# The first projection of a recurrent encoder: 256 of 1024 channels multiplied before the RMSNorm

## The chip, the cores and the metric

The kernel runs on one core of a Trainium2 chip. The time is the device time of one execution in microseconds (us); of the kernel before, three runs were timed, and their median is 829.23 us. All instruction times are read from one profiled execution, counted from the start of its span. The engines are PE (matrix products, with its weight loads listed apart as PEld), DVE (vector), ACT (scalar), POOL (GpSimd) and SP, which issues most of the DMA.

## The reference

One encoder layer over 512 tokens of 1024 channels, float32, with a residual stream `x`:

```python
n = rmsnorm(x, norm_mix)                 # x * rsqrt(mean(x*x) + 1e-6) * norm_mix
proj = n @ w_in + b_in                   # 1024 -> 4624 columns: q, forget gates, values, gates of two head groups
x += concat(hgrn2(proj), mlstm(proj)) @ w_out
x += cross_attention(rmsnorm(x), rmsnorm(mem))
x += square(relu(rmsnorm(x) @ w_up)) @ w_down
out = rmsnorm(x, norm_final)
```

The columns 1536 to 2047 of `proj` are the values of the HGRN2 heads, `v = n @ w_in[:, 1536:2048] + b_in[1536:2048]`. They are computed first, and the change lies in their computation and in what prepares it. Since 1/rms is one number for each token and `norm_mix` one for each channel, `(x * r * g) @ W` equals `r * (x @ (g * W))`, with `r` applied to rows of the result and `g` to rows of `W`; over a part of the channels too.

## The kernel before

**Products.** A float32 product is made of three passes over pairs of rounded tiles: `split_out` lets ACT write the high part of a tile (a rounded copy) and DVE the low part (the tile less its high part); `mm3` then issues high·high, high·low and low·high (lines 261, 262 and 263). Every weight block (128 x 1024, 512 KB) is loaded by SP into one of three buffers `st`, and split by `split(i)` into one of three buffers `wh` and one of three `wl` (line 258: ACT, then DVE). A block can be split only when PE has done its last product with the block three before it.

**The first projection.** The tokens are four tiles of 128 (t = 0 to 3), the channels eight groups of 128 (k). A tile of `x` comes by one DMA of 512 KB. `x_stat(t)` sums its squares (ACT, line 338; for tile 0 half on ACT, half on DVE) and POOL makes 1/rms by a power of -0.5 (line 340). `x_scale(t, g)` multiplies 512 channels by 1/rms and by `gmix[g]` on DVE (line 344); `gmix` is the row `norm_mix` spread over the partitions by PE (`spread`, line 164). `x_turn(t, g)` transposes these four 128 x 128 blocks on PE (line 349) against the identity in `cs`, and `x_split(t, g)` splits the result into `xT` (line 258). `part_v(t, q)` then multiplies two channel groups of tile t by weight block q: 6 matmuls of 512 columns into the accumulator `acc_v[t]`. The last blocks (q = 3) and the bias are outside the hand order: `d = acc_v[t] + bias` on DVE (line 429). `xT` is kept: the gate projection (lines 617, 618) and all later projections of `proj` multiply it as well.

**What sets the order.** Inside `manual_schedule` PE, DVE and ACT take their work in the written order; the calls are interleaved so that one tile's transposes stand between other tiles' products. POOL and SP, and everything after the block, are put in order by the scheduler of the framework. Each engine runs its instructions strictly in that order; an instruction that waits holds all that is behind it. Before the first transposes `keep_busy` issues products of a constant tile (line 160) that nothing reads.

The order before, of which the change rewrites all:

```python
x_stat(0); x_scale(0, 0); x_turn(0, 0); spread(1); split(0); x_split(0, 0); x_stat(1)
part_v(0, 0); x_scale(1, 0); x_turn(1, 0); split(1); x_stat(2); part_v(0, 1); ...
```

Of the kernel before, what the change touches and what calls it, by code (L numbers as in the profile page):

```python
# [39 lines left out]
C_ID, C_MF, C_MB, C_SEL, NC1 = 0, 128, 256, 384, 392  # L40
# [40 lines left out]
def trunk(ctx: ExitStack, tc: tile.TileContext, x, mem, wpk, vec, cst, lmask, rmask, rows, out):  # L81
    nc = tc.nc
# [4 lines left out]
    v, sc, gp, pe = nc.vector, nc.scalar, nc.gpsimd, nc.tensor  # L87
# [33 lines left out]
    cs = sb.tile([P, NC1], F32, name="cs")  # L121
# [19 lines left out]
    def behind(a, b):  # L141

        tc.add_manual_dep(a.ins, b.ins.name, mybir.DependencyInfo(mybir.DependencyClass.NoSync, mybir.DependencyReason.DATA),
                          reason="order of an engine")

    def load_x(t):
        nc.sync.dma_start(out=xtile[t], in_=x[t * P:t * P + P, :])

    row_load = nc.scalar.dma_start(out=grow1[96:97, :], in_=rows[0:1, :])
    load_x(0)  # L150
    behind(nc.scalar.dma_start(out=cs, in_=cst[:, 0:NC1]), row_load)
    for g in range(2):
        v.memset(grow1[0:96, g * 512:g * 512 + 512], 0.0)
    gmix = [smb(), smb()]
    idle = mmb()

    def keep_busy(n):

        for _ in range(n):
            pe.matmul(idle[:, 0:P], lhsT=ones[:, 0:P], rhs=ones[:, 0:P], start=True, stop=True)  # L160

    def spread(g):

        pe.matmul(gmix[g], lhsT=ones[0:97, 0:P], rhs=grow1[0:97, g * 512:g * 512 + 512], start=True, stop=True)

    with tc.manual_schedule(engines={mybir.EngineType.PE}):
        keep_busy(6)
        spread(0)
        keep_busy(4)

    def small_setup():
        lmf = A4()
        nc.sync.dma_start(out=vc, in_=vec)
        nc.sync.dma_start(out=lmf[:, 0:len(LEVELS) * P], in_=lmask)
        for j in range(4):
            a = lmf[32 * j:32 * j + 32, 32 * j:NLV * P]
# [53 lines left out]
    st_tiles, hl_tiles = {}, {}  # L230

    def load(i):
        if i >= NSTREAM or i in st_tiles:
            return
        t = T("st", 1024, 3)
        nc.sync.dma_start(out=t, in_=wpk[i])
        st_tiles[i] = t

    def split(i):
        if i >= NSTREAM or i in hl_tiles:  # L240
            return
        load(i)
        s = st_tiles[i]
        hi, lo = T("wh", 1024, 3, F32R), T("wl", 1024, 3, F32R)
        made = split_out(hi, lo, s)
        hl_tiles[i] = (hi, lo)
        return made[1]
# [9 lines left out]
    def split_out(dst_hi, dst_lo, src):  # L257
        return sc.activation(dst_hi, src, AF.Copy), v.tensor_tensor(out=dst_lo, in0=src, in1=dst_hi.bitcast(F32), op=ALU.subtract)  # L258

    def mm3(ps, ah, al, bh, bl, first, last):  # L260
        pe.matmul(ps, lhsT=ah, rhs=bh, start=first, stop=False)  # L261
        pe.matmul(ps, lhsT=ah, rhs=bl, start=False, stop=False)  # L262
        pe.matmul(ps, lhsT=al, rhs=bh, start=False, stop=last)  # L263
# [50 lines left out]

    xT = XT()
    xs = xk(xT)
    load(0)
    load_x(1)
    load(1)
    load_x(2)  # L320
    load_x(3)
    load(2)
    load(3)

    junk, junk0 = xT[1][:, 0:1025], G4()
    rx, tp = {}, {}

    def x_stat(t):

        ss = tiny(1)  # L330
        if t == 0:
            s0, s1 = tiny(1), tiny(1)
            sc.activation(junk[:, 512:1025], xfull[t][:, 512:1025], AF.Square, scale=1.0 / 32, accum_out=s1)
            xg = xfull[t][:, 0:512]
            v.scalar_tensor_tensor(out=junk0[:, 0:512], in0=xg, scalar=1.0 / D, in1=xg, op0=ALU.mult, op1=ALU.mult, accum_out=s0)
            v.tensor_tensor(out=ss, in0=s0, in1=s1, op=ALU.add)
        else:
            sc.activation(junk, xfull[t], AF.Square, scale=1.0 / 32, accum_out=ss)
        rx[t] = tiny(1)
        gp.tensor_tensor(out=rx[t], in0=ss, in1=nh, op=ALU.pow)  # L340

    def x_scale(t, g):
        xg = xtile[t][:, g * 512:g * 512 + 512]
        v.scalar_tensor_tensor(out=xg, in0=xg, scalar=rx[t], in1=gmix[g], op0=ALU.mult, op1=ALU.mult)

    def x_turn(t, g):
        tp[t, g] = smb()
        for k in range(4):
            pe.transpose(tp[t, g][:, k * P:k * P + P], xtile[t][:, g * 512 + k * P:g * 512 + k * P + P], ident)

    def x_split(t, g):
        p3 = tp[t, g][:, :].rearrange("p (k t) -> p k t", t=P)
        split_out(ap(xT[g], t * P, [1024, 4], [1, P]), ap(xT[g], 512 + t * P, [1024, 4], [1, P]), p3)

    acc_v = [mmb() for _ in range(4)]

    def part_v(t, q):
        w = hl_tiles[q]  # L360
        for k in range(2):
            kk = 2 * q + k
            z = slice(k * 512, k * 512 + 512)
            mm3(acc_v[t], xs[kk][0][:, t * P:t * P + P], xs[kk][1][:, t * P:t * P + P], w[0][:, z], w[1][:, z], kk == 0, kk == 7)

    ET = mybir.EngineType
    with tc.high_priority(), tc.manual_schedule(engines={ET.PE, ET.DVE, ET.Activation}):
        x_stat(0)
        x_scale(0, 0)
        x_turn(0, 0)  # L370
        spread(1)
        split(0)
        x_split(0, 0)
        x_stat(1)
        part_v(0, 0)
        x_scale(1, 0)
        x_turn(1, 0)
        split(1)
        x_stat(2)
        part_v(0, 1)  # L380
        x_split(1, 0)
        x_scale(2, 0)
        part_v(1, 0)
        x_turn(2, 0)
        x_stat(3)
        x_scale(3, 0)
        part_v(1, 1)
        x_turn(3, 0)
        x_scale(0, 1)
        x_split(2, 0)  # L390
        x_scale(1, 1)
        part_v(2, 0)
        x_split(3, 0)
        x_turn(0, 1)
        split(2)
        part_v(2, 1)
        x_split(0, 1)
        x_turn(1, 1)
        x_scale(2, 1)
        part_v(3, 0)  # L400
        x_split(1, 1)
        x_scale(3, 1)
        part_v(3, 1)
        x_turn(2, 1)
        x_split(2, 1)
        part_v(0, 2)
        x_turn(3, 1)
        x_split(3, 1)
        part_v(1, 2)
        part_v(2, 2)  # L410
        split(3)
        part_v(3, 2)
        small_setup()


    vh = []

    def bias_row(i):
        b = T2()
# [3 lines left out]
    bvh = bias_row(0)  # L423
    load(4)
    load(5)
    for t, ps in enumerate(acc_v):
        part_v(t, 3)
        d = VV()
        v.tensor_tensor(out=d[:, 0:512], in0=ps, in1=bvh[:, 0:512], op=ALU.add)
        vh.append(d)  # L430


    ys = [None] * 8
# [1029 lines left out]
```

## Time and profile before

| | us |
|---|---|
| median of three timed runs (lowest, highest) | 829.23 (829.09, 829.29) |
| profiled execution, its own time | 829.61 |
| its span from first to last instruction | 827.6 |
| PE busy in the span | 814.7 |
| DVE, ACT, POOL busy | 590.6, 435.2, 77.7 |
| first transposes of `x` on PE start | 7.36 |
| the ten small products of line 656 start on PE | 54.20 |

The page gives busy time by engine, the chain of work that ended last (followed back from the last instruction to what released it), and groups of instructions. The timeline lists single instructions: start, duration, engine, line, operation, tiles, shape; in brackets the idle time before it and what ended that. A PE matmul of the timeline lasts longer than it holds the engine, since the next one starts before it has drained: what counts for throughput is the distance from start to start. The products of line 656 serve as a mark below: the same work stands ahead of them on PE in both kernels, apart from what the change adds, and from there on all engines have the same instructions in the same order.

### The profile page before, as it was taken

The numbers are of one execution on the slowest core, as the hardware profiler recorded it, in microseconds if no ns is written. First come the engines' busy times: TensorE is split into PE (matmuls) and PEld (weight loads), VectorE is DVE, ScalarE is ACT, GpSimd is POOL, SyncE is SP. The second block draws the span as 40 slices with busy tenths as digits, with TensorE's granted clock in tenths as the row PEclk, the third lists the DMA queues.
The fourth block names the chain that finished last, engine by engine and source line by source line (L and its number), as shares of the span: only waits on it lengthen the run. The fifth ranks groups of instructions, "written<-read, shape, count | busy, mean of one in ns | idle before, by whom it ended". The sixth has DMA issues, their size and how long they took to land.

```text
span 827.6 us, 12644 instructions
## 1 busy us (share of the span) xinstructions
PE 814.7 (98%) x4862; PEld 677.0 (82%) x4862; DVE 590.6 (71%) x1046; ACT 435.2 (53%) x791; POOL 77.7 (9%) x131
## 2 busy tenths in 40 slices
PE   8999999999999999999999999999999999999996
PEld 6788778877878988887888888888888888888885
DVE  6568975699479888545668985676568566756685
ACT  5247574546578485445455575443454345434544
POOL 2000000100010000100100004012102210220001
PEclk9999999999999999999999999999999999999998
DMA  7332223322342334532343349969836982798332
GB/s 277 118 116 94 78 79 104 101 88 81 102 128 77 128 128 152 148 96 89 106 124 72 83 126 305 254 166 272 224 101 182 280 207 94 187 295 204 105 74 101
DMA packets 34125, 118.91 MB, mean 144 GB/s; under 512 B 3921, under 2 KB 4049, under 8 KB 34066
## 3 DMA queue, kind: packets, MB, share of 16 engines
q1 hardware_dynamic: 22832, 77.80, 27.6%
q0 software_dynamic: 10944, 39.85, 21.7%
q8 instruction: 38, 0.62, 0.3%
q10 hardware_dynamic: 290, 0.47, 0.2%
q14 instruction: 21, 0.17, 0.1%
HBM read 116.00 MB, written 2.10 MB: 143 GB/s over the span
## 4 chain that ended last, share of the span: by engine, by line
PE 85%; issue 6%; DVE 5%; ACT 2%; DMA 1%; POOL 1%; POOLq 0%; ACTq 0%; DVEq 0%
PE mm L261 17%; PE mm L263 17%; PE mm L262 17%; PE sm L1154 6%; PE sm L1155 6%; PE sm L1153 6%; PE mm L1154 2%; PE mm L1153 2%; PE mm L1155 2%; PE sm L827 1%; DVE wl L258 1%; PE sm L562 1%; PE sm L485 1%; ACT wh L258 1%; PE sm L263 1%
## 5 line engine op out<-in xcount | busy, mean ns | idle before, releaser
L258 ACT ACTIVATE wh<-st 128x1024 fp32r<-128x1024 f32 x131 | 138.7, 1060 | 185.0 <-PE mm L262 117.4
L261 PE MATMUL mm<-xT,wh 128*128 128x512 f32 x544 | 215.5, 397 | 0.0
L258 DVE TENSOR_TENSOR wl<-st,wh 128x1024 fp32r<-128x1024 f32 x131 | 160.1, 1223 | 77.3 <-ACT wh L258 76.8
L263 PE MATMUL mm<-xT,wl 128*128 128x512 f32 x544 | 212.9, 391 | 0.1
L262 PE MATMUL mm<-xT,wh 128*128 128x512 f32 x544 | 212.5, 391 | 0.2 <-DVE xT L975 0.2
L263 PEld LDWEIGHTS mm<-xT,wl 128*128 128x128 f32 x544 | 102.2, 188 | 21.8 <-DVE wl L258 0.3
L262 PEld LDWEIGHTS mm<-xT,wh 128*128 128x128 f32 x544 | 102.3, 188 | 20.8 <-DVE xT L975 0.9
L261 PEld LDWEIGHTS mm<-xT,wh 128*128 128x128 f32 x544 | 102.2, 188 | 20.8 <-ACT wh L258 0.3
L1102 POOL DMA_DIRECT2D as<-in_wpk x52 | 39.6, 763 | 250.0 <-DVE wl L258 165.0
L1342 DVE SCALAR_TENSOR_TENSOR t<-mm,rg 128x512 f32<-128x512 f32 x32 | 22.0, 690 | 52.2 <-PE mm L263 52.0
L1155 PE MATMUL sm<-wh,yT 128*128 128x512 f32 x128 | 49.8, 389 | 0.0
L1154 PE MATMUL sm<-wl,yT 128*128 128x512 f32 x128 | 49.8, 389 | 0.0
L1153 PE MATMUL sm<-wh,yT 128*128 128x512 f32 x128 | 49.8, 389 | 0.0
L258 ACT ACTIVATE wh<-as 128x1024 fp32r<-128x1024 f32 x26 | 27.6, 1062 | 37.0 <-PE sm L1155 23.7
L258 DVE TENSOR_TENSOR wl<-as,wh 128x1024 fp32r<-128x1024 f32 x26 | 31.9, 1225 | 14.0 <-ACT wh L258 14.0
L1153 PE MATMUL sm<-wh,a 128*128 128x512 f32 x84 | 32.9, 391 | 0.0
L1155 PE MATMUL sm<-wh,a 128*128 128x512 f32 x84 | 32.7, 390 | 0.0
L1154 PE MATMUL sm<-wl,a 128*128 128x512 f32 x84 | 32.7, 389 | 0.0
L1285 DVE TENSOR_TENSOR vv<-vv,sm 128x512 f32<-128x512 f32 x48 | 31.0, 680 | 1.7 <-PE sm L1155 1.7
L199 POOL TENSOR_TENSOR tiny<-tiny,misc 128x4 f32<-128x4 f32 (+1 forms) x10 | 9.6, 963 | 201.9 <-DVE tiny L197 136.7
L1153 PEld LDWEIGHTS sm<-wh,yT 128*128 128x128 f32 x128 | 24.0, 188 | 5.0
L1155 PEld LDWEIGHTS sm<-wh,yT 128*128 128x128 f32 x128 | 24.0, 188 | 5.0
(329 smaller groups left out, 1572.4 us busy)
## 6 DMA issues: line engine op xcount, KB each, us to landing
st<-in_wpk SPq DMA_DIRECT2D x131, 512.0 KB, 3.4
as<-in_wpk POOLq DMA_DIRECT2D x52, 512.0 KB, 6.5
gate<-in_wpk POOLq DMA_DIRECT2D x24, 512.0 KB, 7.2
as<-in_x SPq DMA_DIRECT2D x4, 512.0 KB, 6.7
vv<-in_x SPq DMA_DIRECT2D x8, 256.0 KB, 3.9
out<-vv SPq DMA_DIRECT2D x7, 256.0 KB, 2.2
a<-in_mem SPq DMA_DIRECT2D x2, 512.0 KB, 3.8
t<-in_rows SPq DMA_DIRECT2D x2, 256.0 KB, 5.6
```

The costliest lines, as they stand in the source:

```text
L199: gp.tensor_tensor(out=r, in0=ms, in1=nh.to_broadcast([P, w]), op=ALU.pow)
L258: return sc.activation(dst_hi, src, AF.Copy), v.tensor_tensor(out=dst_lo, in0=src, in1=dst_hi.bitcast(F32), op=ALU.subtract)
L261: pe.matmul(ps, lhsT=ah, rhs=bh, start=first, stop=False)
L262: pe.matmul(ps, lhsT=ah, rhs=bl, start=False, stop=False)
L263: pe.matmul(ps, lhsT=al, rhs=bh, start=False, stop=last)
L485: mm = pe.matmul(ps[b * i:b * i + b, z:z + b], lhsT=kc[j][:, w * P + b * i:w * P + b * i + b], rhs=rhs(j, w * P, i), start=True, stop=True)
L1102: return gp.dma_start(out=dst, in_=wpk[idx], **kw)
L1153: pe.matmul(ps, lhsT=ah, rhs=bh, start=new, stop=False, **fl)
L1154: pe.matmul(ps, lhsT=ah, rhs=bl, start=False, stop=False, **fl)
L1155: pe.matmul(ps, lhsT=al, rhs=bh, start=False, stop=end and k == 1, **fl)
L1285: added = v.tensor_tensor(out=z, in0=z, in1=ps, op=ALU.add if sign > 0 else ALU.subtract)
L1342: v.scalar_tensor_tensor(out=y, in0=ps, scalar=0.0, in1=rrow[:, 0:512], op0=ALU.max, op1=ALU.mult)
```

## The change

Channels 0 to 255 are no longer normed before they are multiplied for `v`. `x` comes in other pieces: the first 256 channels of two tiles at a time (256 KB each), with the two halves of weight block 0 between them, then the other 768 channels of each tile. Raw channels of tile pairs are transposed (`pair_turn(i, 0)`) and split (`pair_split(i, 0)`). Weight block 0 is multiplied by `norm_mix` while it is split (`gained`), with the column `gcol` made by two PE products of one column. All four tiles are multiplied by it at once (`part_a`, 24 matmuls, accumulators `acc_a`). `keep_a(t)` multiplies these sums by 1/rms on DVE, POOL adds the bias, and the accumulators of the other three weight blocks are added at the end. Channels 256 to 1023 are normed, transposed and split as before. Since the later projections need the normed channels 0 to 255 too, these are scaled (4 x 128 x 256), transposed (8 more 128 x 128 blocks) and split a second time, at the end of the block, into the same place of `xT`. Of `cs` only the identity (64 KB) is loaded at the start. `keep_busy` shrinks from 10 products to 4.

```diff
+    def load_first(i):
+        nc.sync.dma_start(out=ap(xin[i], 0, [1280, 2], [1, 256]), in_=x[2 * i * P:2 * i * P + 2 * P, 0:256].rearrange("(t p) c -> p t c", p=P))
+    def load_rest(t):
+        nc.sync.dma_start(out=xtile[t][:, 256:1024], in_=x[t * P:t * P + P, 256:1024])
...
-    behind(nc.scalar.dma_start(out=cs, in_=cst[:, 0:NC1]), row_load)
+    behind(nc.scalar.dma_start(out=ident, in_=cst[:, C_ID:C_ID + P]), row_load)
...
-        keep_busy(6)
-        spread(0)
         keep_busy(4)
+        for k in range(2):
+            pe.matmul(idle[:, 256 + k:257 + k], lhsT=grow1[0:97, k * P:k * P + P], rhs=ones[0:97, 0:1], start=True, stop=True)
+        spread(1)
+    sc.activation(gcol, idle[:, 256:258], AF.Copy)
...
     def x_stat(t):
         ss = tiny(1)
...
+        sc.activation(junk, xfull[t], AF.Square, scale=1.0 / 32, accum_out=ss)
         rx[t] = tiny(1)
         gp.tensor_tensor(out=rx[t], in0=ss, in1=nh, op=ALU.pow)
...
+    def gained(k):
+        z = slice(k * 512, k * 512 + 512)
+        hi, lo, w, g = hl_tiles[0][0][:, z], hl_tiles[0][1][:, z], st_tiles[0][:, z], gcol[:, k:k + 1]
+        sc.activation(hi, w, AF.Copy, scale=g)
+        v.scalar_tensor_tensor(out=lo, in0=w, scalar=g, in1=hi.bitcast(F32), op0=ALU.mult, op1=ALU.subtract)
...
+    def keep_a(t):
+        vh.append(VV())
+        v.tensor_scalar(out=vh[t][:, 0:512], in0=acc_a[t], scalar1=rx[t], scalar2=None, op0=ALU.mult)
...
+        pair_turn(0, 0)
+        spread(0)
+        pair_turn(1, 0)
+        gained(0)
+        pair_split(0, 0)
+        pair_split(1, 0)
+        gained(1)
+        for k in range(2):
+            for t in range(4):
+                part_a(t, k)
+        x_stat(0)
+        x_stat(1)
+        x_scale(0, 2, 2)
+        keep_a(0)
+        x_scale(1, 2, 2)
+        pair_turn(0, 2)
+        split(1)
+        pair_split(0, 2)
+        keep_a(1)
+        part_v(0, 1)
+        part_v(1, 1)
+        x_stat(2)
+        x_stat(3)
+        x_scale(2, 2, 2)
+        x_scale(0, 4, 4)
+        x_turn(0)
+        keep_a(2)
+        x_scale(3, 2, 2)
+        pair_turn(1, 2)
+        keep_a(3)
+        x_scale(1, 4, 4)
+        pair_split(1, 2)
+        part_v(2, 1)
...
+        for t in range(4):
+            x_scale(t, 0, 2)
         part_v(2, 2)
+        pair_turn(0, 0)
+        pair_split(0, 0)
         part_v(3, 2)
+        pair_turn(1, 0)
+        pair_split(1, 0)
...
+    for t in range(4):
+        gp.tensor_tensor(out=vh[t][:, 0:512], in0=vh[t][:, 0:512], in1=bvh[:, 0:512], op=ALU.add)
+    for t in range(4):
         part_v(t, 3)
+        v.tensor_tensor(out=vh[t][:, 0:512], in0=acc_v[t], in1=vh[t][:, 0:512], op=ALU.add)
```

On POOL, the powers that make 1/rms. Before, the four stand one behind the other (line 340; `tiny` are the sums and the results, one per tile):

```order
L340 TENSOR_TENSOR tiny_131<-tiny_125,misc 128x1
L340 TENSOR_TENSOR tiny_148<-tiny_146,misc 128x1
L340 TENSOR_TENSOR tiny_168<-tiny_166,misc 128x1
L340 TENSOR_TENSOR tiny_192<-tiny_190,misc 128x1
L741 MEMSET vv_2049 128x4
```

Now (line 344 is the power, line 469 the addition of the bias row `t_55` to a kept sum `vv`):

```order
L344 TENSOR_TENSOR tiny_171<-tiny_169,misc 128x1
L344 TENSOR_TENSOR tiny_175<-tiny_173,misc 128x1
L344 TENSOR_TENSOR tiny_210<-tiny_208,misc 128x1
L469 TENSOR_TENSOR vv_178<-vv_178,t_55_345 128x512
L469 TENSOR_TENSOR vv_192<-vv_192,t_55_345 128x512
L344 TENSOR_TENSOR tiny_214<-tiny_212,misc 128x1
L469 TENSOR_TENSOR vv_223<-vv_223,t_55_345 128x512
```

Two of the additions have come to stand ahead of the power of tile 3.

On ACT, the end of the block, up to the gate projection's bias (line 620 before, 662 now). `xT_106` and `xT_103` hold channels 512 to 1023, `xT_102` the others; `wh` rows are weight blocks. Before:

```order
L258 ACTIVATE xT_106<-sm_269 128x4x128
L258 ACTIVATE wh_288<-st_116 128x1024
L258 ACTIVATE wh_355<-st_319 128x1024
L182 ACTIVATE tiny_305<-tiny_305 128x8
L258 ACTIVATE wh_359<-st_321 128x1024
L620 ACTIVATE a_64_389<-mm_372,vc 128x512
```

Now:

```order
L265 ACTIVATE wh_289<-st_116 128x1024
L265 ACTIVATE wh_383<-st_347 128x1024
L265 ACTIVATE xT_103<-sm_284 128x4x128
L265 ACTIVATE xT_102<-sm_305 128x2x256
L265 ACTIVATE wh_387<-st_349 128x1024
L265 ACTIVATE wh_393<-st_391 128x1024
L265 ACTIVATE xT_102<-sm_318 128x2x256
```

The split of the second pair's channels 0 to 255 (`sm_318`) stands behind the splits of the next two weight blocks.

On PE, at that place, the last products of the values (`mm_250`), the transposes of that pair (line 365) and the first of the gate projection (lines 659, 660; `wh_383` is its weight block, `mm_425` and `mm_497` belong to the two projections after it). Now:

```order
L270 MATMUL mm_250<-wh_289,xT_103 128x512
L365 MATMUL sm_318<-cs,as_72 128x128 x4
L659 MATMUL mm_400<-xT_102,wh_383 128x512
L268 MATMUL mm_425<-xT_102,wh_387 128x512
L268 MATMUL mm_497<-xT_102,wh_393 128x512
L660 MATMUL mm_400<-xT_102,wh_383 128x512
L659 MATMUL mm_400<-xT_102,wh_383 128x512
```

Before, products of the values stood there, and the gate's rows (line 617) followed them directly, with products of tiles 2 and 3 left over for later.

More of the change, by code (lines that the diff above doesn't have):

```diff
@@ L144, in behind @@
                           reason="order of an engine")
-    def load_x(t):
-        nc.sync.dma_start(out=xtile[t], in_=x[t * P:t * P + P, :])
+    def load_first(i):
+        nc.sync.dma_start(out=ap(xin[i], 0, [1280, 2], [1, 256]), in_=x[2 * i * P:2 * i * P + 2 * P, 0:256].rearrange("(t p) c -> p t c", p=P))
+    def load_rest(t):
+        nc.sync.dma_start(out=xtile[t][:, 256:1024], in_=x[t * P:t * P + P, 256:1024])
     row_load = nc.scalar.dma_start(out=grow1[96:97, :], in_=rows[0:1, :])
-    load_x(0)
-    behind(nc.scalar.dma_start(out=cs, in_=cst[:, 0:NC1]), row_load)
+    load_first(0)
+    behind(nc.scalar.dma_start(out=ident, in_=cst[:, C_ID:C_ID + P]), row_load)
     for g in range(2):
@@ L164, in spread @@
         pe.matmul(gmix[g], lhsT=ones[0:97, 0:P], rhs=grow1[0:97, g * 512:g * 512 + 512], start=True, stop=True)
+    gcol = misc[:, 58:60]
     with tc.manual_schedule(engines={mybir.EngineType.PE}):
-        keep_busy(6)
-        spread(0)
         keep_busy(4)
+        for k in range(2):
+            pe.matmul(idle[:, 256 + k:257 + k], lhsT=grow1[0:97, k * P:k * P + P], rhs=ones[0:97, 0:1], start=True, stop=True)
+        spread(1)
+    sc.activation(gcol, idle[:, 256:258], AF.Copy)
     def small_setup():
@@ L173, in small_setup @@
         nc.sync.dma_start(out=vc, in_=vec)
+        nc.sync.dma_start(out=cs[:, P:NC1], in_=cst[:, P:NC1])
         nc.sync.dma_start(out=lmf[:, 0:len(LEVELS) * P], in_=lmask)
@@ L316, in trunk @@
     xs = xk(xT)
-    load(0)
-    load_x(1)
+    st_tiles[0] = T("st", 1024, 3)
+    for k in range(2):
+        nc.sync.dma_start(out=st_tiles[0][:, k * 512:k * 512 + 512], in_=wpk[0][:, k * 512:k * 512 + 512])
+        if k == 0:
+            load_first(1)
+    load_rest(0)
+    load_rest(1)
     load(1)
-    load_x(2)
-    load_x(3)
+    load_rest(2)
+    load_rest(3)
     load(2)
     load(3)
-    junk, junk0 = xT[1][:, 0:1025], G4()
+    junk = xT[1][:, 0:1025]
     rx, tp = {}, {}
@@ L330, in x_stat @@
         ss = tiny(1)
[L331 to L338, printed above, removed]
+        sc.activation(junk, xfull[t], AF.Square, scale=1.0 / 32, accum_out=ss)
@@ L339, in x_stat @@
         rx[t] = tiny(1)
         gp.tensor_tensor(out=rx[t], in0=ss, in1=nh, op=ALU.pow)
[L342 to L347, printed above, removed]
-        for k in range(4):
[L349 to L353, printed above, removed]
@@ L357, in trunk, with x_scale, x_turn, x_split @@
-    acc_v = [mmb() for _ in range(4)]
+    def x_scale(t, k, n):
+        xg = xtile[t][:, k * P:(k + n) * P]
+        v.scalar_tensor_tensor(out=xg, in0=xg, scalar=rx[t], in1=gmix[k // 4][:, k % 4 * P:(k % 4 + n) * P], op0=ALU.mult, op1=ALU.mult)
+    def x_turn(t):
+        tp[t] = smb()
+        for k in range(4):
+            pe.transpose(tp[t][:, k * P:k * P + P], xtile[t][:, 512 + k * P:640 + k * P], ident)
+    def x_split(t):
+        p3 = tp[t][:, :].rearrange("p (k t) -> p k t", t=P)
+        split_out(ap(xT[1], t * P, [1024, 4], [1, P]), ap(xT[1], 512 + t * P, [1024, 4], [1, P]), p3)
@@ new lines, in pair_turn, with pair_split @@
+    def pair_turn(i, k0):
+        tp[i, k0] = smb()
+        for k in range(2):
+            for u in range(2):
+                z = k * 256 + u * P
+                pe.transpose(tp[i, k0][:, z:z + P], xtile[2 * i + u][:, (k0 + k) * P:(k0 + k) * P + P], ident)
+    def pair_split(i, k0):
+        o = k0 * 1024 + i * 256
+        split_out(ap(xT[0], o, [1024, 2], [1, 256]), ap(xT[0], 512 + o, [1024, 2], [1, 256]),
+                  tp[i, k0][:, :].rearrange("p (k t) -> p k t", t=256))
+    hl_tiles[0] = T("wh", 1024, 3, F32R), T("wl", 1024, 3, F32R)
@@ new lines, in gained, with part_a @@
+    def gained(k):
[3 more added lines that the diff above has]
+        v.scalar_tensor_tensor(out=lo, in0=w, scalar=g, in1=hi.bitcast(F32), op0=ALU.mult, op1=ALU.subtract)
+    acc_a, acc_v, vh = [mmb() for _ in range(4)], {}, []
+    def part_a(t, k):
+        z = slice(k * 512, k * 512 + 512)
+        mm3(acc_a[t], xs[k][0][:, t * P:t * P + P], xs[k][1][:, t * P:t * P + P], hl_tiles[0][0][:, z], hl_tiles[0][1][:, z], k == 0, k == 1)
@@ L359, in part_v @@
+    def keep_a(t):
+        vh.append(VV())
+        v.tensor_scalar(out=vh[t][:, 0:512], in0=acc_a[t], scalar1=rx[t], scalar2=None, op0=ALU.mult)
     def part_v(t, q):
         w = hl_tiles[q]
+        if q == 1:
+            acc_v[t] = mmb()
         for k in range(2):
@@ L363, in part_v @@
             z = slice(k * 512, k * 512 + 512)
-            mm3(acc_v[t], xs[kk][0][:, t * P:t * P + P], xs[kk][1][:, t * P:t * P + P], w[0][:, z], w[1][:, z], kk == 0, kk == 7)
+            mm3(acc_v[t], xs[kk][0][:, t * P:t * P + P], xs[kk][1][:, t * P:t * P + P], w[0][:, z], w[1][:, z], kk == 2, kk == 7)
     ET = mybir.EngineType
     with tc.high_priority(), tc.manual_schedule(engines={ET.PE, ET.DVE, ET.Activation}):
-        x_stat(0)
-        x_scale(0, 0)
-        x_turn(0, 0)
-        spread(1)
@@ L372, in trunk @@
-        split(0)
-        x_split(0, 0)
+        pair_turn(0, 0)
[5 more added lines that the diff above has]
+        gained(1)
+        for k in range(2):
+            for t in range(4):
+                part_a(t, k)
+        x_stat(0)
         x_stat(1)
-        part_v(0, 0)
-        x_scale(1, 0)
-        x_turn(1, 0)
+        x_scale(0, 2, 2)
+        keep_a(0)
+        x_scale(1, 2, 2)
+        pair_turn(0, 2)
         split(1)
+        pair_split(0, 2)
@@ L379, in trunk @@
+        keep_a(1)
+        part_v(0, 1)
+        part_v(1, 1)
         x_stat(2)
[L380 to L384, printed above, removed]
-        x_stat(3)
[L386 to L394, printed above, removed]
-        split(2)
-        part_v(2, 1)
-        x_split(0, 1)
-        x_turn(1, 1)
@@ L399, in trunk @@
[L399 to L405, printed above, removed]
+        x_stat(3)
+        x_scale(2, 2, 2)
[8 more added lines that the diff above has]
+        part_v(2, 1)
+        x_turn(1)
+        x_split(0)
+        part_v(3, 1)
+        split(2)
+        x_split(1)
@@ L406, in trunk @@
+        x_scale(2, 4, 4)
         part_v(0, 2)
-        x_turn(3, 1)
-        x_split(3, 1)
+        x_turn(2)
+        x_scale(3, 4, 4)
+        x_split(2)
         part_v(1, 2)
+        x_turn(3)
+        split(3)
+        x_split(3)
+        for t in range(4):
+            x_scale(t, 0, 2)
         part_v(2, 2)
-        split(3)
+        pair_turn(0, 0)
+        pair_split(0, 0)
         part_v(3, 2)
+        pair_turn(1, 0)
+        pair_split(1, 0)
         small_setup()
-    vh = []
     def bias_row(i):
@@ L425, in trunk @@
     load(5)
-    for t, ps in enumerate(acc_v):
+    for t in range(4):
+        gp.tensor_tensor(out=vh[t][:, 0:512], in0=vh[t][:, 0:512], in1=bvh[:, 0:512], op=ALU.add)
+    for t in range(4):
         part_v(t, 3)
-        d = VV()
-        v.tensor_tensor(out=d[:, 0:512], in0=ps, in1=bvh[:, 0:512], op=ALU.add)
-        vh.append(d)
+        v.tensor_tensor(out=vh[t][:, 0:512], in0=acc_v[t], in1=vh[t][:, 0:512], op=ALU.add)
     ys = [None] * 8
```

## Prediction

> **What bounds the kernel now.** I read the page's first and fourth part, then the windows, then the chain in order of time.
>
> ```profile
> PE 814.7 (98%) x4862; PEld 677.0 (82%) x4862; DVE 590.6 (71%) x1046; ACT 435.2 (53%) x791; POOL 77.7 (9%) x131
> PE 85%; issue 6%; DVE 5%; ACT 2%; DMA 1%; POOL 1%; POOLq 0%; ACTq 0%; DVEq 0%
> 0.00:50.00 50.00, 47.76 (x214) 37.09 (x215) 32.79 (x69) 21.95 (x32) 4.65 (x21) 1.00 0.48 174
> 50.00:100.00 50.00, 49.96 (x470) 40.31 (x469) 38.54 (x73) 28.43 (x39) 0.16 (x2) 1.00 0.33 106
> 100.00:150.00 50.00, 50.00 (x465) 41.88 (x464) 33.13 (x65) 29.75 (x70) 1.02 (x1) 1.00 0.30 99
> ```
>
> PE is the bound (first number after the window's length: its busy time), and after the head it hardly stops until 150 us. So what the head costs PE arrives at the end unchanged, and the question is when PE reaches the mark at 54.20, where the ten products of line 656 start.
>
> ```profile
> 0.74 0.52 ACTq L149
> 1.37 5.85 DMA cs<-in_cst
> 7.36 0.64 PE sm L349 x4
> ...
> 10.98 1.23 DVE wl L258
> 12.26 0.50 PE mm L262
> ...
> 54.20 1.20 PE L656 MATMUL sm<-tiny,a 128*128 128x32 f32 x10
> ```
>
> The chain begins with the constants (196 KB), which land at 7.22 and let the first transposes start at 7.36; from 12.26 on it is PE.
>
> **The work of PE up to the mark.** Rates come from the timeline:
>
> ```profile
> 13.07 0.40 PE L262 MATMUL mm<-wl,xT 128*128 128x512 f32 x1
> 13.30 0.40 PE L263 MATMUL mm<-wh,xT 128*128 128x512 f32 x1
> 31.57 0.47 PE L617 MATMUL mm<-xT,wh 128*128 128x512 f32 x1
> 53.74 0.39 PE L262 MATMUL mm<-xT,wh 128*128 128x512 f32 x1
> 53.97 0.39 PE L263 MATMUL mm<-xT,wl 128*128 128x512 f32 x1
> 15.09 0.44 PE sm L349 x4
> 3.72 1.92 PE L164 MATMUL sm<-rg,t 97*128 97x512 f32 x2
> 7.82 1.02 PE L164 MATMUL sm<-rg,t 97*128 97x512 f32 x2
> ```
>
> A 512-column matmul holds PE 0.23 us in the values' part and 0.227 later (starts 13.07 to 13.30, 53.74 to 53.97); four transposes 0.44; a `spread` 0.86 late (7.82 to the next product at 8.67) and 1.71 early (3.72 to 5.43, where the next row quoted further down starts). From 7.36 to the mark stand 96 products for the values, 76 of the gate and the next two and a half projections, 32 transposes, four more of line 627, and one spread: 96 x 0.232 + 76 x 0.227 + 9 x 0.44 + 0.86 = 44.3 us. The time that passes is 54.20 - 7.36 = 46.8, so PE waits 2.5 us. About 1.7 of that lies before 12.84 (three waits for DVE), the rest is small, such as 0.45 at 31.1 to 31.6. The hand order hides the rest. The change must be judged by this: start + work + waits.
>
> **Start.** PE begins with `keep_busy`:
>
> ```profile
> 1.00 2.93 PE L160 MATMUL mm<-t 128*128 128x128 f32 x12 [1.00 <-POOL as L138]
> 5.43 0.42 PE L160 MATMUL mm<-t 128*128 128x128 f32 x1
> 6.76 0.28 PE L160 MATMUL mm<-t 128*128 128x128 f32 x1
> 4.50 0.69 DVE L335 SCALAR_TENSOR_TENSOR gate<-as 128x512 f32<-128x512 f32 x1 [2.56 <-DMA as<-in_x]
> 5.92 1.06 ACT L258 ACTIVATE wh<-st 128x1024 fp32r<-128x1024 f32 x1 [0.63 <-DMA st<-in_wpk]
> ```
>
> The first 512 KB are there at 4.50, the next at 5.92, so pieces of 256 KB should come near 3.7, 4.4, 5.1 and 5.8, and the 64 KB identity among them near 4.9. The DMA is then not what starts PE. Before, the row `norm_mix` was used at 3.72, the moment `keep_busy` ended; I let it be there at 3.4. Then come the two one-column products for `gcol`, four passes, of a form that the trace lacks: nothing, or as much as `keep_busy`'s 0.23 a pass (12 passes from 1.00 to 3.72), 0.9 in all. Their weight loads are full size, so I take 0.9: `spread(1)` starts at 4.3, ends at 6.0, and the first pair is turned at 6.0 instead of 7.36: **-1.4**. (With nothing for them: -2.2.)
>
> **Clock.** The same pass of `keep_busy` takes 0.42 at 5.43 and 0.28 at 6.76: PE ran at half rate until about 6.5, after 5.5 us of unbroken work, though the windows print 1.00 throughout. The new head breaks that work: PE idles from 2.8 (8 passes) to 3.4. Counting from 4.3, full rate comes between 6.6 (as before) and 10 (5.5 us later); I take about 8. Then the first turn costs 0.42 more and `spread(0)` 0.85 more: **+1.3**; 0.4 with 6.6, and with 10 also half of the first products, 2.1. [...]
>
> **More work.** Channels 0 to 255 are turned twice: 8 transposes, **+0.9**. The four scalings of 256 columns, the four `keep_a` and the second splits are on DVE and ACT; they count only where PE waits for them:
>
> **Waits.** A product that follows its transposes directly waits for ACT, then DVE:
>
> ```profile
> 7.36 0.63 PE L349 MATMUL sm<-cs,as 128*128 128x128 f32 x4 [0.32 <-DMA cs<-in_cst]
> 8.02 0.60 ACT L258 ACTIVATE xT<-sm 128x512 fp32r<-128x512 f32 x1 [1.04 <-PE sm L349]
> 8.65 0.69 DVE L258 TENSOR_TENSOR xT<-sm,xT 128x512 fp32r<-128x512 f32 x1 [0.41 <-ACT xT L258]
> 8.51 1.05 ACT L338 ACTIVATE xT<-as 128x1025 fp32r<-128x1025 f32 x1
> 9.73 0.55 POOL L340 TENSOR_TENSOR tiny<-tiny,misc 128x1 f32<-128x1 f32 x1 [3.62 <-ACT xT L338]
> 10.32 0.75 DVE L344 SCALAR_TENSOR_TENSOR as<-as,tiny,sm 128x512 f32<-128x512 f32 x1 [0.98 <-POOL tiny L340]
> 10.98 1.22 DVE L258 TENSOR_TENSOR wl<-st,wh 128x1024 fp32r<-128x1024 f32 x1
> 9.55 1.05 ACT L258 ACTIVATE wh<-st 128x1024 fp32r<-128x1024 f32 x1
> 14.22 0.53 POOL L672 MEMSET a<- 128x512 f32 x1
> 8.63 0.43 SPq L420 DMA_DIRECT2D t<-in_rows  x1
> ```
>
> From the first transpose the high part is usable after 1.31 us (7.36 to 8.62, and 0.05), so PE, busy 0.44 of it, waits 0.87; the low part is ready 0.74 after that, two products (0.46) later, so 0.28 more: 1.15 for a **bare handover**. Before, every such handover but the first stood behind other products.
>
> The 24 products of `part_a` need no wait: the first start at 9.0 (6.0, two turns, one spread, at the clock above), the gained halves of the weights are split by then or during them. They end at 14.6.
>
> *First handover*, `pair_turn(0, 2)` at 14.6: tiles 0 and 1 are scaled by 13 (their sums stand behind `gained(1)` on ACT, from 9.8 and 10.9, and 8.51 to 10.32 is 1.81 from a sum's start to the scaling). `part_v(0, 1)` follows it directly: **1.15**.
>
> *Second handover*, `pair_turn(1, 2)`: the sums of tiles 2 and 3 stand on ACT behind the split of the first handover, at 15.8 and 16.8. POOL makes 1/rms of tile 2 at 17.0 to 17.5, but then the two additions of 128 x 512 come ahead of tile 3's. The trace has no such addition: at least the 0.53 of the memset of that shape, at most 0.55 for an instruction of one column plus 0.53 for each of two operands and the result, 2.1; as one memset and one DVE pass of two operands (0.69) I take 1.2. (The bias they wait for, issued at 8.63 before, is now behind more loads, but there by 15 or 16.) Tile 3's 1/rms is then ready at 17.5 + 2.4 + 0.6 = 20.5, and its 256 columns, half of 0.75, at 21.0. PE has done `part_v(0, 1)` and `part_v(1, 1)` and `x_turn(0)` at 19.4, so it waits **1.6** (0.4 were the additions free, as DVE is busy with `x_scale(0, 4, 4)` and `keep_a(2)` until 19.2; 3.4 with 2.1 each), and `part_v(2, 1)` follows directly, **1.15** again. [...]
>
> After that other products stand between turns and uses, as before; DVE's backlog leaves 0.1.
>
> *Third handover*, at the gate: let E be the end of the values' last product. PE turns the second pair (0.44) and the gate's first product needs it. On ACT, however, the split of the second next weight block stands ahead; its buffer comes free with that same last product. It runs from E + 0.2 for 0.96, the pair's split 0.6 after it: E + 1.8, a wait of **1.35**. Three products of high parts take 0.7. The low part stands on DVE behind two blocks' low parts (1.22 each) and the last addition of 0.69, the second block only after ACT: E + 0.2 + 1.05 at best, in fact the first from E - 0.1, the addition, the second until E + 3.0, the pair's until E + 3.65, another **1.15**.
>
> **Sum.** -1.4 + 1.3 + 0.9 + 1.15 + 2.75 + 0.1 + 2.5, less the old waits of 2.5: **+4.8 us**. The profiled execution of 829.61 would become 834.4; the median of the runs shown is 0.4 below it, so I predict **834.0**.
>
> **Rivals.** 0.2% is 1.7 us, about what a measurement of this kernel tells from no change. (a) Forecast, 834.0, chance 0.45. (b) The additions on POOL are near the memset's 0.53 and tile 3 is not late: 1.2 less, 832.8; 0.20. For it: POOL's busy share is 9% and its additions have time; against: they stand in the one place where PE looks to POOL. (c) Half rate until 10 or later: 0.8 to 1.2 more, 834.8 to 835.2; 0.18. [...] For it: the broken work of the head; against: the early products of `spread` are long and may count. (d) The first pieces or the identity land late (more, smaller pieces; the constants needed 5.85 us before) and the start stays at 7.3: 1.3 more, of which the clock gives back 0.9 as PE is then at full rate: 834.4 to 835.3; 0.07. (e) Faster or equal: the long run of 24 products lets ACT and DVE get ahead, and none of the three handovers is bare. Then only start, clock and work are left: -1.4 + 1.3 + 0.9 - 2.5 = -1.7, 827.5. It decides when the new waits fall below 2.5 in all. For it: DVE and ACT have 71% and 53%; against: each user stands right behind its transposes on PE, whatever the others have done. 0.10, half of it only as far as no change.
>
> **Range and chances.** From (b) with full rate at 6.6 (0.9 less than there, 831.9), and a bit for the start at its lower bound, to 836.2, with additions of 1.6 us or the latest clock: 831.2 to 836.2. Slower 0.89, the same 0.06 (half of (e) and the fringe of (b)), faster 0.05.
>
> **What would show it.** In the changed profile: the first transposes near 6.0; a second spread or turn at half rate after 6.6; 24 products without a gap to about 14.6; PE idle for ACT about 0.9 us twice before 25; POOL's additions of line 469 between the third and fourth power, with DVE waiting for POOL at the scaling of tile 3; PE idle twice before line 660, first for ACT, then for DVE; the products of line 698 (656 before) near 59.0. I am wrong if these come at or before 54.2, or if they come late and the end does not.

## The result: 837.21 us, slower by 0.9%

| | before | changed |
|---|---|---|
| median (lowest to highest), five runs each, us | 829.22 (829.09 to 829.29) | 837.21 (835.15 to 838.15) |
| profiled execution, us | 829.61 | 837.57 |
| its span, us | 827.6 | 835.6 |
| mark: the ten products of line 698 (656 before) start | 54.20 | 61.95 |

The ratio is 1.0091, 95% interval 1.0080 to 1.0101. The forecast of 834.0 had the sign and most of the mechanism; 3 us are missing. All of them lie before the mark: from the mark to the end of the execution it is 829.61 - 54.20 = 775.41 us before and 837.57 - 61.95 = 775.62 now.

The page of the changed kernel looks as the old one did, PE busy for 98%:

```profile
PE 819.0 (98%) x4862; PEld 679.5 (81%) x4862; DVE 594.7 (71%) x1054; ACT 437.5 (52%) x795; POOL 82.4 (10%) x135
```

Its timeline shows the steps of the forecast one by one: the head, the first handover, the second with POOL and DVE ahead of it, the third at the gate, and the mark.

```profile
3.01 0.98 PE L173 MATMUL mm<-t,rg 97*128 97x1 f32 x4
5.70 1.06 PE L365 MATMUL sm<-cs,as 128*128 128x128 f32 x4
6.55 1.91 PE L167 MATMUL sm<-rg,t 97*128 97x512 f32 x2
8.26 0.94 PE L365 MATMUL sm<-cs,as 128*128 128x128 f32 x4
...
14.52 0.60 PE L365 MATMUL sm<-cs,as 128*128 128x128 f32 x4
15.80 0.50 PE L268 MATMUL mm<-wh,xT 128*128 128x512 f32 x1 [0.69 <-ACT xT L265]
...
17.38 2.52 POOL L469 TENSOR_TENSOR vv<-vv,t 128x512 f32<-128x512 f32 x2
19.38 0.27 PE L365 MATMUL sm<-cs,as 128*128 128x128 f32 x1
19.87 0.54 POOL L344 TENSOR_TENSOR tiny<-tiny,misc 128x1 f32<-128x1 f32 x1
20.44 0.48 DVE L348 SCALAR_TENSOR_TENSOR as<-as,tiny,sm 128x256 f32<-128x256 f32 x1 [1.20 <-POOL tiny L344]
20.98 0.55 PE L365 MATMUL sm<-cs,as 128*128 128x128 f32 x3 [1.32 <-DVE as L348]
22.21 0.50 PE L268 MATMUL mm<-wh,xT 128*128 128x512 f32 x1 [0.69 <-ACT xT L265]
23.53 0.63 PE L268 MATMUL mm<-wh,xT 128*128 128x512 f32 x1
...
39.73 0.60 PE L365 MATMUL sm<-cs,as 128*128 128x128 f32 x4
40.89 0.58 ACT L265 ACTIVATE xT<-sm 128x512 fp32r<-128x512 f32 x1
41.52 0.50 PE L659 MATMUL mm<-xT,wh 128*128 128x512 f32 x1 [1.19 <-ACT xT L265]
43.26 0.79 PE L660 MATMUL mm<-xT,wh 128*128 128x512 f32 x1 [0.78 <-DVE xT L265]
44.28 0.63 PE L660 MATMUL mm<-xT,wh 128*128 128x512 f32 x1
...
61.95 1.20 PE L698 MATMUL sm<-tiny,a 128*128 128x32 f32 x10
```

Two rows were not expected: a product lasts 0.63 us at 23.53 and again at 44.28, where 0.39 is usual, and the next one starts 0.427 us later instead of 0.23. PE is back at half rate. The windows say when (columns: stretch, its length, PE's busy time and instructions, granted clock, DMA share, GB/s):

```profile
15.76:19.17 3.41, 3.37 (x15) 1.00 0.81 271
19.17:22.59 3.42, 1.41 (x10) 1.00 0.19 75
22.59:26.00 3.41, 3.41 (x11) 0.50 0.04 7
...
36.24:39.66 3.42, 3.42 (x18) 1.00 0.04 18
39.66:43.07 3.41, 1.63 (x8) 1.00 0.36 83
43.07:46.48 3.41, 3.22 (x8) 0.50 0.83 265
```

The granted clock is full from 8.93 for 13.65 us, half for 3.41, full for 17.07, half for 3.41, then full to the last microseconds: 4, 1, 5 and 1 times 3.413 us. (In the first 8.93 us the windows view prints 1.00 too, but there the distances from start to start are those of half rate: four transposes take 0.85 us at 5.70 and 0.43 at 18.95.) Each half-rate window follows one in which PE was busy for less than half: 1.41 of 3.41 us (41%) in the second handover, 1.63 (48%) in the third. Eleven instructions fit into the first of them, where 18 fit into the next (26.00 to 29.41). Half of its busy time is lost in each, less what PE would still have waited: by an estimate from these rows about 1.6 us, 3.2 together. That is the missing part.

### The profile page after: what moved, and what is told of

Read it like the earlier page. It is cut to its first block, busy times and chain, and to the rows that moved or that the text cites. A ratio compares the mean times of both kernels' runs of the same rounds, so it can differ in the third digit from the quotient of the medians.

```text
span 835.6 us, 12665 instructions
## 1 busy us (share of the span) xinstructions
PE 819.0 (98%) x4862; PEld 679.5 (81%) x4862; DVE 594.7 (71%) x1054; ACT 437.5 (52%) x795; POOL 82.4 (10%) x135
## 4 chain that ended last, share of the span: by engine, by line
PE 84%; issue 6%; DVE 5%; ACT 2%; POOL 1%; DMA 1%; POOLq 0%; DVEq 0%; ACTq 0%
PE mm L268 17%; PE mm L270 17%; PE mm L269 17%; PE sm L1195 6%; PE sm L1197 6%; PE sm L1196 6%; PE mm L1195 2%; PE mm L1197 2%; PE mm L1196 2%; PE sm L869 1%; PE sm L604 1%; PE sm L527 1%; DVE wl L265 1%; ACT wh L265 1%; PE sm L270 1%
## 5 line engine op out<-in xcount | busy, mean ns | idle before, releaser
L1197 PEld LDWEIGHTS sm<-wh,yT 128*128 128x128 f32 x128 | 24.0, 188 | 5.0
L1144 POOL DMA_DIRECT2D gate<-in_wpk x24 | 18.2, 757 | 101.0 <-DVE wl L265 64.3
```

Of the source, the lines that this page charges most:

```text
L1144: return gp.dma_start(out=dst, in_=wpk[idx], **kw)
L1197: pe.matmul(ps, lhsT=al, rhs=bh, start=False, stop=end and k == 1, **fl)
```

## The experiments

Theory from here on, drawn from the two pairs of windows above: a window of 3.41 us in which PE idles for more than half of its time is followed by one at half rate. By it the waits that the change makes are paid twice, once as waits and once in the clock. The windows of the other kernels are counted on in steps of 3.413 us from where their full rate begins. Rivals: the waits alone cost the whole 8 us and the half rate is a coincidence of the time; or the rate depends on something other than PE's idling. Each group of four or two was timed against the kernel before on one chip, where that took 829.11, 828.89 and 829.00 us (medians), against 829.22 beside the changed kernel: differences between kernels of different groups are uncertain by some 0.3 us.

**PE kept busy in its waits.** Products that nothing reads, with every wait left in place (the nine at the gate stand in one place, right behind the turn):

```diff
+    def fill(z, n):
+        for _ in range(n):
+            pe.matmul(z[:, 0:P], lhsT=ident, rhs=ident, start=True, stop=True)
...
+        acc_v[2] = mmb()
+        fill(acc_v[2], 12)
         pair_turn(1, 2)
+        fill(acc_v[2], 5)
...
         pair_turn(1, 0)
+        fill(tp[0, 0], 9)
         pair_split(1, 0)
```

> The changed kernel with 26 more 128x128 products on PE whose results nothing reads: twelve ahead of the turn of tiles 2 and 3 for the second handover, five behind it, six and three in the two waits at the gate. Nothing else is moved; every wait stays as long, but PE works in most of it. Theory (PE's idle time in a 3.4 us window drops its clock to half for the next window): no half rate behind the head, products 0.23 us apart throughout, the mark (first product of the ten of line 698) near 58.8 instead of 61.95, and 837.2 - 3.2 = 834.0 us, within 0.8. Rival (the clock falls there for another reason, or the waits alone cost the 8 us): the same two stretches at half rate, the mark at 62, 837.2 us, within 1.

Measured: 835.72 us (835.51 to 836.89), ratio 1.0083 (1.0069 to 1.0096). No window at half rate was left between the head and 62 us (the granted clock is 1.00 in all of them), but only half of the time came back. The profile says why: a float32 product of this size is two entries of 0.113 us, where a transpose is one of 0.11.

```profile
19.05 2.87 PE L402 MATMUL mm<-cs 128*128 128x128 f32 x24
59.94 1.20 PE L706 MATMUL sm<-tiny,a 128*128 128x32 f32 x10
```

From 19.05 on twelve of them take 2.7 us in a wait of 1.5. So it was run again with six, three and six:

> The first of these kernels again with fewer of the products that nothing reads. There they took 0.226 us each, not the 0.11 of a transpose that their number was reckoned with, so that twelve and five overran the second handover by about 1.3 us. Now six and three stand there (1.36 and 0.68 us, for waits of 1.5 and 0.8) and six at the gate, so that no wait is longer than in the changed kernel. Theory (idle windows drop the clock): no half rate behind the head, all of the 3.2 us back: 834.0 us, within 0.8 for where the head's window falls. Rival (waits alone): 837.2 us.

Measured: 834.62 us (833.82 to 835.42), ratio 1.0069 (1.0055 to 1.0082), 2.6 below the changed kernel. The mark comes at 58.93, 3.0 earlier, and the forecast had 59.0 for it.

```profile
19.32 1.50 PE L402 MATMUL mm<-cs 128*128 128x128 f32 x12
41.77 0.50 PE L668 MATMUL mm<-xT,wh 128*128 128x512 f32 x1 [0.78 <-DVE xT L265]
58.93 1.20 PE L706 MATMUL sm<-tiny,a 128*128 128x32 f32 x10
```

The waits are still there, the work is more, and the kernel is faster. The place of the windows does not explain it: one begins at 19.33 here, where the changed kernel has one from 19.17, and the window from there to 22.74 is now 99% busy instead of 41%. That shows the second payment, and its size; the waits alone do not cost 8 us.

**The waits taken away.** First the one for POOL: its additions go behind the last power.

```diff
-        gp.tensor_tensor(out=vh[t][:, 0:512], in0=vh[t][:, 0:512], in1=bvh[:, 0:512], op=ALU.add)
+        behind(gp.tensor_tensor(out=vh[t][:, 0:512], in0=vh[t][:, 0:512], in1=bvh[:, 0:512], op=ALU.add), powers[3])
```

> The changed kernel with its four bias additions on POOL ordered behind the power of tile 3, so that this power no longer stands behind two of them. Theory: the second handover's wait falls by about 1.25 us (one addition's 1.26 for which DVE and PE wait), PE's busy share in its window rises from 41% to nearly 80%, and the stretch at half rate from 22.59 goes too: 837.2 - 1.3 - 1.6 = 834.3 us. Rival (the additions cost only the wait, the clock falls whatever the waits are): 835.9 us. If the additions were not what tile 3's scaling waits for: 837.2 us.

Measured: 833.13 us (832.36 to 833.73), ratio 1.0049 (1.0037 to 1.0062).

```profile
18.52 0.55 POOL L344 TENSOR_TENSOR tiny<-tiny,misc 128x1 f32<-128x1 f32 x1 [0.76 <-ACT xT L342]
19.04 3.76 POOL L469 TENSOR_TENSOR vv<-vv,t 128x512 f32<-128x512 f32 x3
58.09 1.20 PE L698 MATMUL sm<-tiny,a 128*128 128x32 f32 x10
```

More came back than the theory's 2.9: the gate's wait is as long as ever, but in this execution it left no half-rate window either. This kernel's own windows tell why:

```profile
36.92:40.33 3.41, 2.02 (x10) 1.00 0.19 49
40.33:43.74 3.41, 2.84 (x12) 1.00 0.87 290
```

The border at 40.33 falls into the wait and divides it: 59% and 83% busy, and the clock stays at 1.00. A window that began at 37.50 would have been 43% busy (1.45 of 3.41 us, worked out from waits of 1.20 and 0.76). The mean granted clock was 0.998 in all five runs of this kernel, the profiled one among them, so by this none of them had a fall. So the gate's 2.4 us of waits cost 2.4 here, with windows from 36.92 and 40.33, and by the estimate above about 4.0 in the changed kernel, with one from 39.66.

Then the wait at the gate: the second pair's transposes and its split are ordered ahead of the last six products and of the next blocks' splits (`o` is the first product of each half of `part_v(3, 3)`, `'end'` the pair's last transpose, `'act'` its split on ACT, `made[0]` the split of weight block 5 there).

```diff
+            if (t, q) == (3, 3):
+                behind(o, tp[1, 0, 'end'])
...
+        if i == 5:
+            behind(made[0], tp[1, 0, 'act'])
```

> The changed kernel with one order changed at the third handover: the transposes of the second pair and their split stand ahead of the last six products of the first projection and ahead of the splits of the next two weight blocks, so that the six products cover the handover. Theory: both waits at the gate go (2.4 us), and with them the stretch at half rate from 43.07 (1.6): 837.2 - 4.0 = 833.2 us. Rival (waits only): 834.8 us. If the work behind the gate takes the wait over (the next block's split is now later): 836 us or more.

Measured: 833.52 us (833.05 to 833.94), ratio 1.0053 (1.0039 to 1.0067), near the theory's 833.2 and below the rival's 834.8. The third handover has no wait left; the half-rate window behind the second is still there, and the mean granted clock, 0.996 in all five runs, says the same of each.

```profile
38.34 0.60 PE L368 MATMUL sm<-cs,as 128*128 128x128 f32 x4
40.17 0.40 PE L664 MATMUL mm<-xT,wh 128*128 128x512 f32 x1
40.40 0.45 PE L665 MATMUL mm<-xT,wh 128*128 128x512 f32 x1
...
57.95 1.20 PE L703 MATMUL sm<-tiny,a 128*128 128x32 f32 x10
```

Both edits together:

> Both edits before this one together. Theory: 837.2 - 1.3 - 1.6 - 4.0 = 830.3 us with PE's clock at full rate from the head on; what is left over the kernel before (829.2) is the wait of the first handover and what remains of the second, less the earlier start. Rival (waits only): 833.5 us.

Measured: 831.10 us (830.13 to 831.79), ratio 1.0023 (1.0014 to 1.0032): 6.1 of the 8 us are back, where waits alone would have given 3.7. What is short of the forecast, 0.8, is mostly in the head: in the profiled execution the first products are still at half rate, and the fourth starts at 10.41, in the changed kernel at 9.73.

```profile
9.06 0.78 PE L270 MATMUL mm<-wh,xT 128*128 128x512 f32 x1
...
10.41 0.39 PE L270 MATMUL mm<-wh,xT 128*128 128x512 f32 x1
...
55.94 1.20 PE L703 MATMUL sm<-tiny,a 128*128 128x32 f32 x10
```

**The head's clock.** The full rate began at 8.93 in the changed kernel, and at 8.32, 9.61, 9.03 and 10.32 in these four (in the last, products start 0.43 us apart at 9.63 and 0.24 at 10.41), each time behind the first window that has nothing of the one-column products (2.9 to 3.9) in it. In the kernel of both edits, the window from 3.49 to 6.91 had them for 0.4 us only, had one pause of 0.14 us besides, and the next was still at half rate. In the gate edit the window that held all four passes (2.87 to 3.58) was followed by half rate too (a spread takes 1.71 us at 6.28), though the profile counts PE as busy throughout:

```profile
2.20:5.62 3.42, 3.42 (x12) 1.00 1.00 297
```

So the columns were made wide:

```diff
-            pe.matmul(idle[:, 256 + k:257 + k], lhsT=grow1[0:97, k * P:k * P + P], rhs=ones[0:97, 0:1], start=True, stop=True)
+            pe.matmul(idle[:, 256 + k * P:384 + k * P], lhsT=grow1[0:97, k * P:k * P + P], rhs=ones[0:97, 0:P], start=True, stop=True)
-    sc.activation(gcol, idle[:, 256:258], AF.Copy)
+    sc.activation(gcol, ap(idle, 256, [P, 2]), AF.Copy)
```

> The changed kernel with the two products that make the norm weights' columns 128 columns wide instead of one (every column the same, one of them is read); they took 0.21 us a pass at one column already, so they get no longer. Theory (a one-column product leaves PE idle by the clock's reckoning, so that the first window that counts as full begins behind these products): full rate begins one window earlier, between 4.4 and 7.8 us instead of 7.4 to 10.8, and the half-rate part of the head, 1.5 us in the profiled execution, shrinks by 1 to 1.5: 837.2 - 1.2 = 836.0 us with the later drops unchanged. Rival (the head's rate depends on time since the start alone): full rate from about 9 again, 837.2 us.

Measured: 835.23 us (835.05 to 836.11), ratio 1.0078 (1.0065 to 1.0091). Full rate begins at 7.31 and the first product at 8.11 instead of 8.95. This profile does not tell the width from the windows' place: its window from 3.90 to 7.31 begins behind these products (2.87 to 3.72), so narrow ones would have left it as full. The rest of the gain is again in the place of the windows:

```profile
17.55:20.96 3.41, 1.79 (x12) 1.00 0.39 135
20.96:24.38 3.42, 3.00 (x14) 1.00 0.02 5
...
38.03:41.44 3.41, 1.43 (x6) 1.00 0.49 156
41.44:44.86 3.42, 3.42 (x10) 0.50 0.78 248
```

The second handover's worst window is 52% busy, and the next is at 1.00; the gate's is 42% busy, and the next is at 0.50.

> The kernel of both edits (additions behind the last power; re-turn of the second pair ahead of six products) with the wide column products as well. Theory: 831.1 - 1.3 = 829.8 us, with less spread from run to run, because the late and the early start of full rate (830.1 to 831.8) both become an earlier one. Rival (the head's rate depends on time alone): 831.1 us.

Measured: 829.03 us (828.49 to 831.19), ratio 1.0004 (0.9995 to 1.0013): 2.1 less than without the wide columns (1.9 when each is counted from the kernel before on its own chip), more than the 1.3 expected, and no difference from the kernel before. The spread did not shrink. Here too the window ahead of the rise (3.80 to 7.21) begins behind the wide products. What speaks for the width are the times, eleven runs each without a fall behind the head in either profile, and the last kernel below: its window from 0.85 to 4.26 holds all four wide passes (2.86 to 3.71), and full rate begins at 4.26 (four transposes take 0.46 us at 5.06, 0.85 at 5.70 in the changed kernel), so the rate does not depend on time alone.

```profile
0.85:4.26 3.41, 3.26 (x13) 1.00 0.66 178
```

**A version that would beat both.** Three kernels tried to take the waits that are left and the head's half-rate time: two with the head in a new order, the second of them with three products that nothing reads, and one that covers the first two handovers.

> All of the kernel before this one, and the head in another order: the broadcast of the norm weights' second half is halved, one half before the first transposes and one behind the second pair's, that of the first half stands among the first products, the transposes of tiles 0 and 1 for the next two channel blocks stand ahead of the last six of the 24 products, those of tiles 2 and 3 ahead of the last nine products of tiles 1 to 3, and the sums of squares of tile 2 ahead of the pair's split. Theory (every handover is a wait of PE, and PE's time in the head is the time of the kernel): the first handover's 1.2 us goes, of the second's 1.1 some 0.5 stay, the first product starts near 7.2 instead of 9 for 0.85 us of broadcast moved behind it: 829.8 - 1.2 - 0.6 - 0.9 = 827.1 us, faster than the kernel before by 0.2%. Rival (the loads of the rows set the head, not PE): 829 us or more.

Measured: 830.34 us (828.71 to 830.75), ratio 1.0013 (1.0004 to 1.0022): wrong by 3. The profile names three reasons: transposes of tile 0 that I had put too early wait for their scaling, the first rows land later than I had it, so the first product starts at 7.85 instead of 7.2, and the rate is half until 9.97 (products start 0.43 us apart at 9.06 and 9.49), which the theory of the head puts down to two short waits, 0.19 and 0.38 us (the window from 3.15 to 6.56 is 83% busy).

```profile
4.97 1.09 PE L368 MATMUL sm<-cs,as 128*128 128x128 f32 x4 [0.19 <-DMA cs<-in_cst]
6.44 1.12 PE L368 MATMUL sm<-cs,as 128*128 128x128 f32 x4 [0.38 <-DMA as<-in_x]
20.67 0.63 PE L356 MATMUL sm<-cs,as 128*128 128x128 f32 x4 [1.46 <-DVE as L351]
```

> The kernel with the head in another order, mended in two places: the next transposes of tile 0, which had waited 1.5 us for their scaling, stand behind the six products of tile 2, and three products that nothing reads stand in the two waits for the first rows and the identity, so that no window of the head has an idle stretch. Theory (full rate begins behind the first window without one): 830.3 - 1.4 - 1.0 = 827.9 us, faster than the kernel before by 0.1%, and full rate from 7.8 us or earlier. Rival (the head's rate is not lifted by these products): 828.9 us.

Measured: 829.53 us (829.10 to 829.97), ratio 1.0007 (0.9998 to 1.0016). The full rate came at 7.44, as the theory had it (products start 0.23 us apart from 8.34 on), but a new wait of 0.76 us for a weight block's low part stands at 23.58, and the gain was 0.8 instead of 2.4.

> The kernel of both edits with the wide column products, and the first two handovers covered: the first pair's transposes for the next two channel blocks stand ahead of the last three of the 24 products and its split ahead of the sum of squares of tile 2; behind the second pair's transposes stand the next transposes of tile 0. Theory (each handover's wait is PE's own and shrinks by the work put into it): 0.7 to 0.9 us less at the first and 0.4 at the second, 829.0 - 1.2 = 827.8 us, faster than the kernel before by 0.1%. Rival (the wait moves to the next thing that is late, the sums of squares on ACT or the scalings on DVE): 829 us.

Measured: 829.13 us (828.45 to 829.82), ratio 1.0001 (0.9992 to 1.0010). The mark came at 53.63, 0.8 earlier than with both edits and the wide columns, in an execution whose full rate began already at 4.26. The first product started 1.36 earlier (6.74 against 8.10), so behind the head this kernel lost 0.6 of it again; the waits went on to the next late thing, as the rival had it:

```profile
12.44 0.55 PE L368 MATMUL sm<-cs,as 128*128 128x128 f32 x3 [0.55 <-DVE as L351]
18.38 0.50 PE L270 MATMUL mm<-wh,xT 128*128 128x512 f32 x1 [0.25 <-ACT xT L267]
20.51 0.63 PE L356 MATMUL sm<-cs,as 128*128 128x128 f32 x4 [0.20 <-DVE as L351]
53.63 1.20 PE L706 MATMUL sm<-tiny,a 128*128 128x32 f32 x10
```

No version of the change that was run is faster than the kernel before; three cannot be told from it.

## Why the prediction was right, and where it was wrong

| term | forecast | in the profile |
|---|---|---|
| start: first transposes | -1.4 | -1.66 (7.36 to 5.70) |
| clock in the head | +1.3 | +1.5: two turns and a spread take 3.25 us to 8.95, 1.74 at full rate |
| 8 more transposes | +0.9 | +0.9 |
| first handover | +1.15 | +1.2: third product at 16.53 instead of 15.42, the next 0.1 late |
| second handover, with the 0.1 of backlog | +2.85 | +2.6: 1.49 for the scaling (20.98 instead of 19.49), 1.15 for the splits |
| third handover | +2.5 | +2.4: 1.35 (41.52 instead of 40.17) and 1.05 |
| old waits | -2.5 | taken as -2.5 |
| clock falls after the second and third handover | none | +3.2 |
| sum, and the mark | +4.8, 59.0 | +7.65 worked out, 61.95 (+7.75) |

**Right:** the start, the head's rate, the order of what waits for what, and the price of each handover, all within 0.3 us. Rival (b) is out: an addition on POOL took 1.26 us (2.52 for two), 1.2 was taken. Rival (d) is out, the first turns start at 5.70; (e) is out, all three handovers are bare; (c) did not happen in the profiled execution (8.93), though the kernel of both edits shows that it can (10.32). No run shows the 1.2 us of its upper end, 835.2, or the "latest clock" of the range: the six kernels with one-column products came to full rate between 8.32 and 10.32.

**Wrong:** the step "Clock". It dealt with the rate in the head alone, as if PE, once at full rate, stayed there, and so the step "Waits" priced each wait at its length. The clock also fell again, behind two pairs of new waits: 1.49 and 1.15 us of the second handover, 1.35 and 1.05 of the third, each pair within 3.4 us, in windows 41% and 48% busy. By the estimate above it cost 1.6 us twice; with PE kept busy in the same waits the mark is at 58.93 against 59.0 forecast. That it comes so close is in part luck: the other terms were off by up to 0.26 each, in both directions. In the kernel before no window between the head and the mark came under 77%. But the switch near 6.5 us that the prediction read is not the only one in the trace of before: in the last microseconds the rate falls, behind a window 37% busy, and that could have warned. The last two rows are this fall:

```profile
9.98:13.40 3.42, 2.64 (x13) 1.00 1.02 413
818.95:822.36 3.41, 1.27 (x6) 1.00 0.66 246
822.36:825.77 3.41, 0.00 (x0) 0.50 0.72 274
```

The range took in a later rise, but no second fall, and ended 1 us under the median.

The traces of both kernels show the same step between the changes of the clock: from 6.57 to 822.36 in the kernel before are 239 windows of 3.413 us, from 46.48 to 831.55 in the changed one 230. The longest single wait here is 1.49 us, and windows that were 41%, 42% and 48% busy were followed by a clock of 0.50.

The spread of the changed kernel's runs fits this as well: 837.21 to 838.15 with a mean granted clock of 0.993 or 0.994, and 835.15 and 835.27 with 0.996. One window at half rate less is 1.7 of 836 us, 0.002 in the mean clock, and about 1.6 us. The windows of these two runs were not recorded, so for them this is argued, not shown.

## What to carry to other kernels

Where PE is the bound, as here, price a new wait not only by its length: twice PE's idle time filled more than half of a window of 3.41 us (41% and 48% busy), and each time the clock cost, by the estimate above, 1.6 us more. The idle time meant is the profile's, which is less than the waits by start times: 2.0 against 2.6 us in the second handover, where a product's row lasts 0.39 us and the next starts after 0.23. The first handover's 1.2 us of waits stood alone, in windows 81% and 99% busy (12.34 to 15.76 to 19.17), and the clock stayed at 1.00; the second's stood next to each other, and it did not. In a wait that can't be avoided, products that nothing reads were worth having where their measured length fitted: six, three and six took 2.6 us off. In all three handovers the user of a turn stood right behind it, and PE waited 0.69, 0.69 and 1.19 us for ACT, so look for products to order between the two before such a change is judged: two edits of order alone took 6 of the 8 us back.

## What the runs showed of the hardware that was not expected

In the traces of both kernels the changes of PE's granted clock lie whole multiples of 3.413 us apart (239 in the kernel before; 4, 1, 5, 1 and 230 in the changed one), counted from 6.57 us in the first and 8.93 in the second. All windows between the head and the mark that were under 75% busy:

| kernel | window, us | PE busy | clock in the next window |
|---|---|---|---|
| changed | 19.17 to 22.59 | 41% | 0.50 |
| gate edit | 19.27 to 22.68 | 41% | 0.50 |
| wide columns | 38.03 to 41.44 | 42% | 0.50 |
| changed | 39.66 to 43.07 | 48% | 0.50 |
| wide columns | 17.55 to 20.96 | 52% | 1.00 |
| POOL edit | 36.92 to 40.33 | 59% | 1.00 |
| first new head | 16.80 to 20.21 | 71% | 1.00 |

So in these executions the clock fell behind the windows up to 48% busy, as the profile counts it, and stayed behind those from 52% up. In the last microseconds it fell behind a window 37% busy in the kernel before (818.95 to 822.36) and behind one with no product at all in the changed one (828.13 to 831.55).

In the head, a window with 0.4 us of one-column products and a pause of 0.14 in 3.42 was followed by half rate (3.49 to 6.91, both edits), one with a single pause of 0.24 us by full rate (3.80 to 7.21, both edits with wide columns). A product of one column in float32 held PE as long as one of 128 columns, 0.21 us a pass at half rate (four passes from 3.01 to 3.85 in the changed kernel, from 2.87 to 3.72 in the one with wide columns). In all six kernels with one-column products the window that held the last of them was followed by half rate. Of the windows that held all four wide passes the one from 0.85 to 4.26 above was followed by full rate, those from 0.48 to 3.90 and from 0.38 to 3.80 (wide columns alone, and with both edits), which begin by about 0.4 us earlier, by half rate. What makes the difference was not shown. The rate rose between 8.32 and 10.32 in the kernels with one-column products and at 7.31, 7.21, 4.26 and 7.44 in four with wide ones; in the fifth (the first new head), at 9.97, behind a window with two pauses.
